# Merge gates of the LRU branch projected between its pairs of tiles, with a new scan cost and other engines for small copies, in a one-core trunk layer on Trainium2

## The chip, the cores and the metric

The kernel runs on one core of one Trainium2 chip. A core has five engines that run their own instruction queues in order: TensorE (PE in the profile; PEld is its weight load), VectorE (DVE), ScalarE (ACT), GpSimd (POOL) and SyncE (SP, which here only issues DMAs). The metric is the device time of one execution in microseconds (us), as the median of several runs. One execution is also recorded by the hardware profiler; its span goes from its first to its last instruction.

## The reference, cut to what matters

One layer of a streaming encoder works on 512 prompt rows and 128 sample rows (8 requests of 16), 640 in all, with 1024 channels, in float32:

```python
x = x + 0.5 * swiglu(rms_norm(x, norm_ffn1), w_ffn1_up, w_ffn1_down)      # d_ff 2816
h = rms_norm(x, norm_mix)
aq, ak, av, hq, hf, hi, hg, lx, lg, ga, gb, gc = split(h @ w_in)          # 10752 columns
A = sliding_window_attention(aq, ak, av)                # per head norms, sinks, caches
B = hgrn2(hq, hf, hi, hg)                               # gated linear recurrence
xc = causal_conv4(lx)                                   # depthwise, width 4
r, ig = sigmoid(xc @ w_a + b_a), sigmoid(xc @ w_x + b_x)     # 16 blocks of 64
a = exp(-8 * r * softplus(-lambda))
hs = scan(h[t] = a[t] * h[t-1] + sqrt(1 - a[t]**2) * (ig * xc)[t])
C = hs * gelu(lg)
merged = sigmoid(ga) * (A @ w_attn_o) + sigmoid(gb) * (B @ w_hgrn_o) + sigmoid(gc) * (C @ w_lru_o)
x = x + merged @ w_out
x = x + 0.5 * swiglu(rms_norm(x, norm_ffn2), w_ffn2_up, w_ffn2_down)
```

The outputs are the new rows, new keys and values, and the new states: of the convolution (its last three inputs), of the LRU (its last `hs`) and of B.

## The kernel before, in words

Activations lie transposed, 128 channels on the partitions and the 640 rows along the free dimension, two halves of 320. A float32 product is made of three matmuls of a rounded format: each operand is split into a high part and a low part (what is left), and high times high, high times low and low times high are summed. RA and RB (16 tiles of 128 x 640 each) hold the high parts (tiles 0 to 7) and the low parts (8 to 15) of whatever is multiplied next.

**A projection** (`proj`, L744 to L756) makes 128 output channels: a DMA on SP brings a weight tile `wr` (three slots); ACT or DVE casts it to `wh` (L750, two slots); DVE subtracts to `wl` (L751, two slots); then 48 matmuls of 320 columns (8 k-tiles, three parts, two halves; 24 where there are four k-tiles) go to two of four `pp` banks of PSUM, which DVE evacuates. Weight tiles get their slots strictly in the order in which the projections are issued in the program.

**The order of all work** is planned while the program is built. Every operation is entered in program order with its candidates of engines and a cost each, in us (`dve`, `act`, `pol`, L356 to L362). It gets a rank: the number of the current item (each `proj` raises it by 1, each `pair` by 2) plus `S.late`, ties by program order; `wr`, `wh` and `wl` rank at item minus 4, 2 and 1.5. `Sched.run` (L265) then repeatedly takes the engine whose next operation can start first by the estimated costs and gives it, among the operations that could start within 0.04 us of that, the one of lowest rank. The result is a fixed instruction order for each engine; on the chip each engine follows it and waits for its inputs.

**The stages**: first feed-forward (`ffn`, L891); attention with the gates `ga` (`attention`), and its merge, 8 projections with `w_attn_o`; the LRU branch (`lru`, L1169); the HGRN branch (`hgrn`, L1256, eight heads); `w_out`; second feed-forward.

**The feed-forward** works in chunks of the 22 tiles of d_ff: 4, 6, 6 and 6. The first chunk uses plain projections: four tiles of gate and value (8 projections), then 8 down projections of four k-tiles. The other chunks use `pair`, a form with 7 products instead of 8, which needs sums and differences of the normed input: `combos` (L777). A first part of these is entered after tile 0 with `S.late = 4` (L909 to L911). The second part, `rest()` (L812), writes over RA (or RB in the second feed-forward), so it must follow the last of the 8 up projections. It is entered at L912 to L913, right ahead of the 8 down projections, with no lateness: eight splits (a cast on ACT and a subtraction on DVE each, 128 x 640) and two subtractions.

**The LRU branch** treats eight tiles in four pairs. The four first tiles of `lx` are projected during attention. For each pair: projections of `lx` where missing; convolution on DVE (`xc`); the small copies to `CB`, which gathers the states to be output (L1192, L1193); splits, and 12 small matmuls a tile (`me`) against the block weights; sigmoids, exp and tanh on ACT; sqrt on ACT and products on DVE; the scan on DVE (L1227), entered in the plan at the cost of an elementwise operation over 640 elements; two more small copies to `CB` (L1229, L1230). Then, tile by tile, the `lg` projection, gelu on ACT, the product with `hs` and its split into RB (L1232 to L1237). After the last pair the states are transposed and put out, five merge gates are projected (`gate`, L947: a projection, a product with the norm's scale, a sigmoid, in one of six `mgC` slots), then the three projections of the first HGRN head (`heads(0)`), then the merge (L955): 8 projections with `w_lru_o`, the remaining three gates entered between them.

The small copies to `CB` may go to POOL or DVE (L1192, L1193, L1229, L1230). In an HGRN head, four copies of a 32 x 160 tile into the attention matrix may go to ACT or POOL (L1347).

Of the kernel before, what the change touches and what calls it, by code (L numbers as in the profile page):

```python
# [13 lines left out]
ALU = mybir.AluOpType  # L14
# [331 lines left out]
def trunk_kernel(ctx: ExitStack, tc: tile.TileContext, A: dict, O: list):  # L346
# [544 lines left out]
    def ffn(wu, wd, norm, R, H, sfx, done, aside=()):  # L891
        ops = None
        for f0, nf in CHUNKS:
            for f in range(nf):
                for at, job in aside:
                    if at == f0 + f:
                        job()
                if f0:
                    g, u = pair(wu, f0 + f, ops, sfx)
                else:  # L900
                    late = not sfx and f < 2
                    g = scaled("fA" + sfx, proj(wu, 0, KD, f * P, R), late)
                    fn(g.v, g.v, AF.Silu)
                    u = scaled("fB" + sfx, proj(wu, 0, KD, FF + f * P, R), late)
                tt(u.v, g.v, u.v, ALU.mult)
                parts(H, f, u.v)
                if f0 + f == ASIDE:
                    S.late = LATE
                    ops, rest = combos(norm, R, sfx)  # L909
                    S.late = 0.0  # L910
            if f0 == 0:  # L911
                rest()  # L912
            for m in range(KD):  # L913
                ps = proj(wd, f0 * P, nf, m * P, H)
                for o, p in halves(xk(m), ps):
                    stt(o, p, 0.5, o, ALU.mult, ALU.add)
                if f0 + nf == 22:
                    done(m)
# [247 lines left out]
    def smp(v):  # L1166
        return v[:, TP:T].r("p (b t) -> p b t", b=NB)

    def lru():  # L1169
        bds = [S.buf("bd") for _ in range(2)]  # L1170
        for b in bds:
            fill(b.v, 0.0)
        for j in range(4):
            xcs, rs, igs, las, lts = [], [], [], [], []
            for i in range(2):
                m = 2 * j + i
                y = early[m] if m < len(early) else branch(m)
                bd = bds[i]
                for w, nm_ in ((0, "lru_w_a"), (1, "lru_w_x")):
                    for h in range(2):  # L1180
                        a, b = h * 64, h * 64 + 64
                        dma(bd[a:b, w * P + a:w * P + b].at((w, h)), A[nm_][0, 2 * m + h])
                xc = S.buf("lc")
                fn(xc.v, y.v, AF.Identity, scale=prm(CVW + 24 + m), bias=prm(CVB + m))
                for t in range(3):
                    s = 3 - t
                    w = prm(CVW + t * 8 + m)
                    stt(xc[:, s:TP], y[:, 0:TP - s], w, xc[:, s:TP], ALU.mult, ALU.add)
                    stt(smp(xc.v)[:, :, s:], smp(y.v)[:, :, :SB - s], w, smp(xc.v)[:, :, s:], ALU.mult, ALU.add)
                    hist = HIST[:, m, 0:24].r("p (b j) -> p b j", b=NB)[:, :, t:]  # L1190
                    stt(smp(xc.v)[:, :, :s], hist, w, smp(xc.v)[:, :, :s], ALU.mult, ALU.add)
                cp(CB[:, m, 0:3].at(m), y[:, TP - 3:TP], only=("POOL", "DVE"))  # L1192
                cp(CB[:, m, 3:27].at(m).r("p (b j) -> p b j", b=NB), smp(y.v)[:, :, SB - 3:], only=("POOL", "DVE"))  # L1193
                r, ig = S.buf("lr"), S.buf("li")
                for h, l, x in ((BH.v, BL.v, bd.v), (NH.v, NL.v, xc.v)):
                    cp(h, x, only=("ACT",))
                    tt(l, x, h.cast(F32), ALU.subtract)
                for w, o, bias in ((0, r, BA), (1, ig, BX)):
                    for q in range(2):
                        ps = S.buf("me")  # L1200
                        mm([(ps[:, :HT], a[:, w * P:(w + 1) * P], hv(b.v)[:, q, :], a is BH and b is NH, a is BL)
                            for a, b in ((BH, NH), (BH, NL), (BL, NH))])
                        fn(hv(o.v)[:, q, :], ps[:, :HT], AF.Sigmoid, bias=prm(bias + m))
                tt(ig.v, ig.v, xc.v, ALU.mult)
                rs.append(r), igs.append(ig)
            hss = []
            for i in range(2):
                m = 2 * j + i
                a, t = S.buf("la"), S.buf("lt")
                fn(a.v, rs[i].v, AF.Exp, scale=der(N8SP, m))  # L1210
                fn(t.v, rs[i].v, AF.Tanh, scale=der(P8SP, m))
                q = rs[i]
                fn(q.v, a.v, AF.Square)
                stt(t.v, q.v, 1.0, t.v, ALU.add, ALU.mult)
                las.append(a), lts.append(t)
            for i in range(2):
                m = 2 * j + i
                a, t, ig = las[i], lts[i], igs[i]
                fn(t.v, t.v, AF.Sqrt)
                tt(t.v, t.v, ig.v, ALU.mult)  # L1220
                a0 = smp(a.v)[:, :, 0]
                sm = HIST[:, m, 24:32].at(m)
                tt(sm, a0, sm, ALU.mult, only=("DVE",))
                tt(smp(t.v)[:, :, 0], smp(t.v)[:, :, 0], sm, ALU.add, only=("DVE",))
                fill(a0, 0.0, only=("DVE",))
                hs = rs[i]
                S.op([dve(T, lambda o=hs.v, a=a.v, t=t.v: nc.vector.tensor_tensor_scan(o(), a(), t(), 0.0, op0=ALU.mult, op1=ALU.add))],  # L1227
                     [a.v, t.v], [hs.v])
                cp(CB[:, m, 27:28].at(m), hs[:, TP - 1:TP], only=("POOL", "DVE"))  # L1229
                cp(CB[:, m, 28:36].at(m), smp(hs.v)[:, :, SB - 1], only=("POOL", "DVE"))  # L1230
                hss.append(hs)
            for i in range(2):  # L1232
                m = 2 * j + i
                g = scaled("lg", proj(W, 0, KD, LG + m * P, RA))
                fn(g.v, g.v, AF.Gelu_apprx_tanh)
                tt(g.v, g.v, hss[i].v, ALU.mult)
                parts(RB, m, g.v)  # L1237
        co = S.buf("co")
        for h in range(2):
            ps = S.buf("ml")  # L1240
            tr([(ps[0:36, i * P:(i + 1) * P], CB[:, 4 * h + i, :], ident.v) for i in range(4)])
            cp(co[0:36, h * 512:(h + 1) * 512], ps[0:36, :], only=("ACT", "DVE"))
        dma(O[5], co[0:3, :])
        dma(O[10], co[3:27, :])
        dma(O[6], co[27:28, :])
        dma(O[11], co[28:36, :])
        more = lambda m: gate(GC, m, "mgC")
        gates = [more(m) for m in range(5)]
        pre.append(heads(0))
        merge(A["w_lru_o"][0], gates, more)  # L1250

# [4 lines left out]
    def hgrn():  # L1256
# [44 lines left out]
        def head(i):  # L1301
# [31 lines left out]
            for h in (2, 4, 8, 16, 32, 64):  # L1333
# [4 lines left out]
                if h < 32:  # L1338
                    mm([(ps[j * 32:j * 32 + 32, t * 16:t * 16 + 16], K[:, t * P + j * 32:t * P + j * 32 + 32],
                         blocks(Q[:, t * P + j * 32:t * P + j * 32 + 32], h)[:, :, 1, :], True, True) for t in range(n // P) for j in range(4)])  # L1340
                    dst = blocks(atc[:, :n // 4], h)[:, :, 1, :]
                    S.op([dve(n // 8, lambda d=dst, k=masks[h][:, :nb // 4, :], q=ps[:, :n // 8].r("p (n h) -> p n h", h=h):
                              nc.vector.copy_predicated(d(), k(), q()))], [ps.v, mk.v, atc.v], [dst])
                    if h == 16:
                        for j in range(4):
                            p = slice(j * 32, j * 32 + 32)
                            cp(a4[p, :, p].at(j), atc[p, :].r("p (t l) -> p t l", t=NT), only=("ACT", "POOL"))  # L1347
                elif h == 32:
                    mm([(ps[j * 32:j * 32 + 32, t * 32:t * 32 + 32], K[:, t * P + j * 32:t * P + j * 32 + 32],
                         Q[:, t * P + j * 32 + 32:t * P + j * 32 + 64], True, True) for t in range(4) for j in (0, 2)])  # L1350
                    for j in (0, 2):
                        p = slice(j * 32, j * 32 + 32)
                        cp(a4[p, 0:4, j * 32 + 32:j * 32 + 64].at((h, j)), ps[p, 0:P].r("p (t l) -> p t l", t=4), only=("ACT",))
                else:
                    mm([(ps[0:64, t * 64:t * 64 + 64], K[:, t * P:t * P + 64], Q[:, t * P + 64:t * P + P], True, True) for t in range(4)])
                    cp(a4[0:64, 0:4, 64:P].at(h), ps[0:64, 0:256].r("p (t l) -> p t l", t=4), only=("ACT",))
# [131 lines left out]
```

## Time and profile before

| what | before |
|---|---|
| median of 3 runs | 1921.0 us (1920.73 to 1923.34) |
| profiled execution, its time | 1923.28 us |
| its span | 1921.5 us |
| instructions | 35215 |
| PE busy | 1898.9 us (99%) |
| DVE busy | 1389.1 us (72%) |
| ACT busy | 735.8 us (38%) |
| POOL busy | 44.3 us (2%) |
| granted PE clock, mean | 0.996 |

In a row of the profile stand the line of the kernel, the engine, the operation, the tile written and the tiles read (`out<-in`), shapes and a count. AR is the arena in which most tiles of a stage lie, RW and RY are regions whose type changes with the stage, `me` and `ml` PSUM banks of small products, NL and NH the low and high part of the tile that is multiplied next, RS the norm's scale. Helpers record each operation under their own line: L369 is any product or sum of two tiles, L383 any fused multiply and add, L393 any activation or table load on ACT, L402 and L403 copies and casts on ACT and DVE, L405 copies on POOL, L438 any matmul. In brackets or after a bar stands idle time of the engine before the row, and what ended it. Matmuls overlap, so the time of one (0.31 us) is longer than the distance between two.

### The profile page before, as it was taken

To read this page: it belongs to the slowest core of one execution; us is meant where nothing else is said; L and a number is where in the kernel's file an instruction comes from. 1 tells how busy PE (TensorE), PEld (TensorE's weight loads), DVE (VectorE), ACT (ScalarE), POOL (GpSimd) and SP (SyncE) were. 2 spreads that over 40 slices of the span, in tenths; PEclk is the share of its full clock that TensorE was granted. 3 is DMA by queue.
4 is the path that set the end of the run, shared out by engine and by line. 5 is a ranking of instruction groups with operands and counts; after the bars stand their busy time and mean duration, and the time that the engine had idled before them with its cause. 6 is when DMAs were issued, how large, how long until landed. Compare 5 with 4: busy or idle time off the path is not lost.

```text
span 1921.5 us, 35215 instructions
## 1 busy us (share of the span) xinstructions
PE 1898.9 (99%) x14654; PEld 1853.0 (96%) x14654; DVE 1389.1 (72%) x2599; ACT 735.8 (38%) x1295; POOL 44.3 (2%) x86
## 2 busy tenths in 40 slices
PE   8999999999999999999999999999999999999999
PEld 8999999999999999999999999999999999999998
DVE  7897685877787773787547778877556978586784
ACT  6343251433478630876002344335112324142340
POOL 2000000000000000020000000000000000000000
PEclk9999999999999999999999999999999999999999
DMA  6232332224321212213222222222322133222322
GB/s 144 66 94 80 93 87 78 75 78 139 102 62 50 62 48 77 61 57 103 77 77 74 84 80 79 79 81 83 122 72 77 56 99 90 87 65 79 99 64 80
DMA packets 303488, 156.89 MB, mean 82 GB/s; under 512 B 21324, under 2 KB 300956, under 8 KB 303328
## 3 DMA queue, kind: packets, MB, share of 16 engines
q1 hardware_dynamic: 302576, 154.58, 27.7%
q8 instruction: 115, 1.88, 0.4%
q0 software_dynamic: 736, 0.06, 0.4%
q14 instruction: 45, 0.37, 0.1%
q10 hardware_dynamic: 16, 0.00, 0.0%
HBM read 143.32 MB, written 10.63 MB: 80 GB/s over the span
## 4 chain that ended last, share of the span: by engine, by line
PE 93%; DVE 4%; ACT 2%; issue 1%; DMA 1%; SPq 0%; ACTq 0%; DVEq 0%
PE pp L438 84%; PE me L438 4%; PE ml L438 3%; PE ml L447 1%; PE me L447 1%; DVE AR L383 1%; ACT AR L393 1%; DVE AR L369 1%; DVE RB L369 0%; DVE AR L1227 0%; ACT L393 0%; DMA RX<-in_x_prompt_dram 0%; DVE wl L751 0%; SPq L417 0%; DVE RA L369 0%
## 5 line engine op out<-in xcount | busy, mean ns | idle before, releaser
L438 PE MATMUL pp<-RA,wh 128*128 128x320 f32 x4192 | 815.0, 314 | 0.3 <-DVE AR L369 0.3
L438 PEld LDWEIGHTS pp<-RA,wh 128*128 128x128 f32 x4192 | 659.1, 189 | 13.1 <-issue 9.7
L438 PE MATMUL pp<-RA,wl 128*128 128x320 f32 x2096 | 490.7, 310 | 4.9 <-DVE wl L751 4.9
L438 PE MATMUL pp<-RB,wh 128*128 128x320 f32 x2016 | 389.0, 310 | 0.9 <-DVE AR L369 0.9
L438 PEld LDWEIGHTS pp<-RA,wl 128*128 128x128 f32 x2096 | 354.7, 188 | 5.9 <-DVE wl L751 5.9
L438 PEld LDWEIGHTS pp<-RB,wh 128*128 128x128 f32 x2016 | 320.4, 188 | 1.5 <-DVE AR L369 1.4
L750 DVE CAST wh<-wr 128x1024 fp32r<-128x1024 f32 (+2 forms) x142 | 89.4, 630 | 237.2 <-PE pp L438 236.5
L438 PE MATMUL pp<-RB,wl 128*128 128x320 f32 x1008 | 241.9, 310 | 1.6 <-DVE wl L751 1.6
L751 DVE TENSOR_TENSOR wl<-wr,wh 128x1024 fp32r<-128x1024 f32 (+2 forms) x196 | 216.7, 1106 | 1.6 <-ACT wh L750 1.0
L836 ACT CAST RW<-AR 128x512 fp32r<-128x512 f32 x180 | 110.4, 621 | 264.9 <-PE pp L438 135.0
L438 PEld LDWEIGHTS pp<-RB,wl 128*128 128x128 f32 x1008 | 172.1, 188 | 1.9 <-DVE wl L751 1.9
L369 DVE TENSOR_TENSOR AR<-AR 128x640 f32<-128x640 f32 (+12 forms) x272 | 140.0, 519 | 28.9 <-ACT AR L393 16.5
L369 DVE TENSOR_TENSOR AR<-pp,AR 128x320 f32<-128x320 f32 x268 | 127.6, 485 | 35.8 <-PE pp L438 32.7
L393 ACT ACTIVATE AR<-AR 128x640 f32<-128x640 f32 (+2 forms) x184 | 110.5, 604 | 96.9 <-DVE AR L369 89.6
L438 PE MATMUL pp<-RX,RW 128*128 128x320 f32 x864 | 138.6, 309 | 0.0
L438 PEld LDWEIGHTS pp<-RX,RW 128*128 128x128 f32 x864 | 129.6, 188 | 0.0
L833 DVE TENSOR_TENSOR RW<-AR,RW 128x512 fp32r<-128x512 f32 x180 | 122.3, 686 | 2.4 <-ACT RW L836 0.9
L393 ACT ACT_TABLE_LOAD x73 | 93.7, 1283 | 2.5 <-PEq L1476 1.4
L402 ACT COPY AR<-me 128x512 f32<-128x512 f32 (+3 forms) x72 | 25.8, 373 | 123.9 <-PE me L447 115.2
L383 DVE SCALAR_TENSOR_TENSOR AR<-pp,AR 128x320 f32<-128x320 f32 x128 | 61.3, 483 | 15.5 <-PE pp L438 15.4
L438 PE MATMUL pp<-RY,RW 128*128 128x320 f32 x432 | 69.2, 309 | 0.0
L750 ACT CAST wh<-wr 128x1024 fp32r<-128x1024 f32 (+1 forms) x54 | 53.7, 994 | 36.9 <-PE pp L438 36.5
(195 smaller groups left out, 1960.7 us busy)
## 6 DMA issues: line engine op xcount, KB each, us to landing
wr<-in_w_in_dram SPq DMA_DIRECT2D x84, 512.0 KB, 3.7
wr<-in_w_ffn_up_dram SPq DMA_DIRECT2D x52, 512.0 KB, 3.8
AR<-in_w_ffn_up_dram SPq DMA_DIRECT2D x36, 512.0 KB, 4.6
wr<-in_w_ffn_down_dram SPq DMA_DIRECT2D x48, 384.0 KB, 3.3
wr<-in_w_ffn_down_dram SPq DMA_DIRECT2D x16, 256.0 KB, 2.8
wr<-in_w_attn_o_dram SPq DMA_DIRECT2D x8, 512.0 KB, 3.7
AR<-in_state_hgrn_dram SPq DMA_DIRECT2D x8, 512.0 KB, 4.7
wr<-in_w_lru_o_dram SPq DMA_DIRECT2D x8, 512.0 KB, 3.8
```

What stands on the lines that cost most here:

```text
L369: alts = [dve(out.n, lambda: nc.vector.tensor_tensor(out(), a(), b(), op=op))]
L383: return S.op([dve(out.n, lambda: nc.vector.scalar_tensor_tensor(out(), a(), ap_of(s), b(), op0=op0, op1=op1), isinstance(s, View))], [a, ...
L393: nc.scalar.activation(out(), a(), func, bias=ap_of(bias), scale=ap_of(scale), **kw)
L402: alts = [act(out.n, lambda: nc.scalar.copy(out(), a()), 0, a), dve(out.n * (1.0 if a.in_psum else 0.5), lambda: nc.vector.tensor_copy(out ...
L438: nc.tensor.matmul(o(), l(), m(), start=s, stop=e)
L447: nc.tensor.transpose(o(), i(), d())
L750: S.op([act(nk * P, lambda: nc.scalar.copy(h(), r())), dve(nk * P * 0.5, lambda: nc.vector.tensor_copy(h(), r()))], [r], [h], lag=2)
L751: S.op([dve(nk * P, lambda: nc.vector.tensor_tensor(l(), r(), h().bitcast(F32), op=ALU.subtract))], [r, h], [l], lag=1.5)
L833: S.op([dve(out.n, lambda: nc.vector.tensor_tensor(out(), a(), b(), op=op))], [a, b], [out], lag=lag)
L836: S.op([act(out.n, lambda: nc.scalar.copy(out(), a()))], [a], [out], lag=lag)
```

## The change

1. Four of the five merge gates leave the place after the last pair: in each pair, after the `lg` tile 0 (`i == 0`) is entered, one gate is entered, ahead of the `lg` projection of tile 1. After the last pair the loop enters what is missing of five, which is one. `more` is defined ahead of the loop for this.
2. The scan's cost in the plan is that of 1280 elements instead of 640. The instruction is the same.
3. The four kinds of `CB` copies may go to ACT or DVE, and the copies of the attention tile in the HGRN heads to ACT or DVE; POOL gets none of these.
4. `rest()` is entered with `S.late = 4` in both feed-forward stages.

```diff
             if f0 == 0:
+                S.late = 4.0
                 rest()
+                S.late = 0.0
...
+        gates, more = [], lambda m: gate(GC, m, "mgC")
         for j in range(4):
...
-                cp(CB[:, m, 0:3].at(m), y[:, TP - 3:TP], only=("POOL", "DVE"))
-                cp(CB[:, m, 3:27].at(m).r("p (b j) -> p b j", b=NB), smp(y.v)[:, :, SB - 3:], only=("POOL", "DVE"))
+                cp(CB[:, m, 0:3].at(m), y[:, TP - 3:TP], only=("ACT", "DVE"))
+                cp(CB[:, m, 3:27].at(m).r("p (b j) -> p b j", b=NB), smp(y.v)[:, :, SB - 3:], only=("ACT", "DVE"))
...
-                S.op([dve(T, lambda o=hs.v, a=a.v, t=t.v: nc.vector.tensor_tensor_scan(o(), a(), t(), 0.0, op0=ALU.mult, op1=ALU.add))],
+                S.op([dve(2 * T, lambda o=hs.v, a=a.v, t=t.v: nc.vector.tensor_tensor_scan(o(), a(), t(), 0.0, op0=ALU.mult, op1=ALU.add))],
                      [a.v, t.v], [hs.v])
-                cp(CB[:, m, 27:28].at(m), hs[:, TP - 1:TP], only=("POOL", "DVE"))
-                cp(CB[:, m, 28:36].at(m), smp(hs.v)[:, :, SB - 1], only=("POOL", "DVE"))
+                cp(CB[:, m, 27:28].at(m), hs[:, TP - 1:TP], only=("ACT", "DVE"))
+                cp(CB[:, m, 28:36].at(m), smp(hs.v)[:, :, SB - 1], only=("ACT", "DVE"))
...
                 parts(RB, m, g.v)
+                if i == 0:
+                    gates.append(more(len(gates)))
...
-        more = lambda m: gate(GC, m, "mgC")
-        gates = [more(m) for m in range(5)]
+        while len(gates) < 5:
+            gates.append(more(len(gates)))
         pre.append(heads(0))
         merge(A["w_lru_o"][0], gates, more)
...
-                            cp(a4[p, :, p].at(j), atc[p, :].r("p (t l) -> p t l", t=NT), only=("ACT", "POOL"))
+                            cp(a4[p, :, p].at(j), atc[p, :].r("p (t l) -> p t l", t=NT), only=("ACT", "DVE"))
```

## The prediction, made before the changed kernel ran

> **What bounds the kernel now.** I read the page's busy line first, then the waits of the TensorE, then a table of stretches, and last the timeline where the waits lie.
>
> ```profile
> PE 1898.9 (99%) x14654; PEld 1853.0 (96%) x14654; DVE 1389.1 (72%) x2599; ACT 735.8 (38%) x1295; POOL 44.3 (2%) x86
> ```
> ```profile
> PE pp L438 <- DVE wl L751: 6.4, 5, 2.4
> PE me L447 <- DMA RX<-in_x_prompt_dram: 4.6, 2, 2.6
> PE me L438 <- DVE NL L369: 2.4, 1, 2.4
> ```
>
> TensorE (PE) is busy 99%, so only its gaps can be won. The largest sum is five waits for `wl`, the low part of a weight tile, which VectorE (DVE) writes; one wait for `NL` has the same length. The waits on DMA belong to the start, which the change leaves alone. What a gap costs is more than its idle time; the table of stretches shows it (columns: length, then busy us and count of PE, PEld, DVE, ACT, POOL; then the granted PE clock).
>
> ```profile
> 63.00:79.00 16.00, 14.41 (x100) 14.14 (x98) 13.38 (x22) 7.53 (x11) 0.00 (x0) 1.00 0.23 66
> 79.00:84.00 5.00, 5.00 (x23) 4.86 (x24) 4.60 (x12) 1.78 (x4) 0.00 (x0) 0.66 0.25 73
> 767.00:893.00 126.00, 120.34 (x792) 117.84 (x791) 100.20 (x188) 102.60 (x134) 18.45 (x26) 0.97 0.21 62
> 791.00:802.00 11.00, 8.22 (x35) 7.33 (x34) 10.76 (x18) 7.76 (x12) 3.72 (x4) 0.69 0.18 51
> 822.00:827.00 5.00, 2.62 (x18) 2.36 (x17) 5.00 (x10) 1.55 (x3) 0.53 (x2) 1.00 0.06 19
> 864.00:868.00 4.00, 3.55 (x21) 2.87 (x21) 4.00 (x9) 2.58 (x4) 2.63 (x3) 1.00 0.35 102
> 912.00:960.00 48.00, 48.00 (x329) 48.00 (x328) 26.32 (x39) 4.76 (x6) 0.00 (x0) 1.00 0.27 77
> 1522.00:1537.00 15.00, 13.28 (x91) 13.03 (x90) 12.34 (x21) 7.60 (x11) 0.00 (x0) 1.00 0.24 68
> 1537.00:1542.00 5.00, 5.00 (x24) 4.85 (x24) 3.48 (x7) 0.00 (x0) 0.00 (x0) 0.66 0.32 94
> ```
>
> 912 to 960 runs without a gap: 48 us for 329 matmuls, 0.1459 us each. At that pace the other stretches lost: 63 to 84, 21 less 123 x 0.1459 = 3.1 us; 1522 to 1542, 20 less 115 x 0.1459 = 3.2; 791 to 802, 11 less 35 x 0.1459 = 5.9; 822 to 827, 2.4; 864 to 868, 0.9. Together 15.5 us: 6.3 in the two feed-forward stages and 9.2 in the LRU stage (all of 767 to 893 lost 126 less 792 x 0.1459 = 10.4, so 1.2 lies in small pieces). The rows of 79 and 1537 are full of busy PE and still lost 1.6 and 1.5: the granted clock was 0.66 there, right after a gap. The Trainium skill's page "TensorE: Matmul & The Clock Gate" (section "What's actually happening") has the clock fall to half after an idle window of about 3.4 us; the gaps here are shorter (2.4 us at most, waits above), so its length does not fit, while its halving does, and by it no fall would be owed to these gaps.
>
> **The LRU stage, gate projections.** The timeline shows why PE starves (first three rows ACT, DVE and PE near the first pair, then the second pair):
>
> ```profile
> 784.39 1.05 ACT L750 CAST wh<-wr 128x1024 fp32r<-128x1024 f32 x1 [0.38 <-PE pp L438]
> 796.30 1.22 DVE L751 TENSOR_TENSOR wl<-wr,wh 128x1024 fp32r<-128x1024 f32 x1
> 794.72 0.64 PE L438 MATMUL me<-NL,BH 128*128 128x320 f32 x1 [2.41 <-DVE NL L369]
> ```
> ```profile
> 815.55 1.04 ACT L750 CAST wh<-wr 128x1024 fp32r<-128x1024 f32 x1
> 817.01 1.48 DVE L1227 TENSOR_TENSOR_SCAN AR<-AR 128x640 f32<-128x640 f32 x1
> 818.87 1.47 DVE L1227 TENSOR_TENSOR_SCAN AR<-AR 128x640 f32<-128x640 f32 x1
> 820.27 1.54 DVE L369 TENSOR_TENSOR AR<-AR 128x640 f32<-128x640 f32 x2
> 822.38 1.55 DVE L369 TENSOR_TENSOR RB<-AR,RB 128x640 fp32r<-128x640 f32 x2
> 824.09 1.22 DVE L751 TENSOR_TENSOR wl<-wr,wh 128x1024 fp32r<-128x1024 f32 x1
> 825.37 0.56 PE L438 MATMUL pp<-RA,wl 128*128 128x320 f32 x2 [2.38 <-DVE wl L751]
> ```
>
> The cast `wh` ends at 785.4, its `wl` starts at 796.3: it stood 11 us behind the first pair's scans, products and the next pair's convolution. At the second pair it waited from 816.6 to 824.1. A projection is 48 matmuls, 48 x 0.1459 = 7.0 us; its successor's weights may be converted only in that time, since there are two `wh` and two `wl`. Cast 1.04 and subtraction 1.22 leave 7.0 - 2.3 = 4.7 us of slack, less than either wait. So the order on DVE, not its amount, makes the gap.
>
> The plan gives a free engine the ready work of the lowest item number; `wl` ranks at its projection's item minus 1.5 (L751), the pair's work at the item reached when it was issued. Counted from the merge before, the fourth projection has `wl` at 2.5 both times. Before, it is LG3, and the second pair's convolution and the first pair's second product (item 2) come ahead; after, it is LG2, and both stand at item 3, behind. The seventh has 5.5: before it is LG4, behind the second pair's products (3 and 4); after, LX4, with one product (4) ahead and one (6) behind. And each pair hands PE 7.0 us more to run.
>
> What this adds is work for DVE and ACT in the stage (not in the kernel):
>
> ```profile
> L393 ACT ACT_TABLE_LOAD x24 | 30.8, 1283 | 0.4
> L751 DVE TENSOR_TENSOR wl<-wr,wh 128x1024 fp32r<-128x1024 f32 x15 | 18.2, 1215 | 0.0
> L369 DVE TENSOR_TENSOR RW<-pp,RS 128x320 f32<-128x320 f32 x3 | 1.4, 479 | 0.0
> L393 ACT ACTIVATE RW<-RW 128x640 f32<-128x640 f32 x1 | 0.7, 742 | 0.0
> L750 DVE CAST wh<-wr 128x1024 fp32r<-128x1024 f32 x6 | 4.2, 692 | 6.2 <-PE pp L438 6.1
> L403 DVE COPY CB<-AR 128x1 f32<-128x1 f32 x1 | 0.2, 153 | 0.0
> L403 DVE COPY CB<-AR 128x8 f32<-128x8 f32 x1 | 0.7, 715 | 0.0
> ```
> ```profile
> 878.68 0.88 PE me L438 x6
> 893.79 1.55 DVE L369 TENSOR_TENSOR RB<-AR,RB 128x640 fp32r<-128x640 f32 x2
> ```
>
> A gate costs DVE 1.215 + 2 x 0.479 + at most 0.692 = 2.9 us, four 11.5. The stage's PE time grows by 28 us and shrinks by the gaps: 126 + 28 - 9 = 145, DVE 100.2 + 11.5 + the copies (below, 4) = 116, 80% against 100.2/126 = 80% before; ACT 102.6 + 4 x 0.742 + up to 8 more table loads x 1.283 (a sigmoid between two gelus) + four casts of 1.04 + copies of 8 at most = 128, 88%. Neither becomes the bound by amount. Also moved: the four weight loads and their SP issues come earlier; the DMA share of 767 to 893 is 0.21, so they cost nothing. One gate (of the five) plus three head projections stay between LG7 and the merge, 4 x 7.0 = 28 us; the last pair's chain ran from its last small matmuls (`me`, to 879.6) to its products in RB (895.3), 16 us, so this cover holds; without it the merge would wait up to 16 us.
>
> **The scan's cost** in the plan (0.066 + 1.042 ns an element) goes from 0.73 to 1.40 us, against 1.48 measured. It adds no instruction; it makes the plan see the burst about as long as it is (two scans were 1.5 us short). I count it with the gates. Of the 9.2 us I take 8.3, leaving one stall of the smallest size (0.9); bounds: 3.3 (the first stays) and 10.4 (all).
>
> **Combinations later.** `rest()` overwrites RA (RB in the second layer half), so it starts when the last up projection has passed, exactly when the first down projections need weights:
>
> ```profile
> 1527.49 2.30 DVE L369 TENSOR_TENSOR RB<-RW,RB 128x640 fp32r<-128x640 f32 x3 [1.36 <-PE pp L438]
> 1531.91 0.42 DVE L750 CAST wh<-wr 128x512 fp32r<-128x512 f32 x1
> 1534.51 0.82 DVE L369 TENSOR_TENSOR AR<-AR 128x640 f32<-128x640 f32 x1
> 1535.98 0.68 DVE L751 TENSOR_TENSOR wl<-wr,wh 128x512 fp32r<-128x512 f32 x1
> 1536.72 0.56 PE L438 MATMUL pp<-RA,wl 128*128 128x320 f32 x2 [1.72 <-DVE wl L751]
> ```
>
> The second `wl` was possible at 1532.3 and came at 1536.0, behind four combination steps and others. With rank item + 4 the combinations stand behind the next weights. `wl` at 1532.3 to 1533.1 ends before PE needs it (1536.72 - 1.72 = 1535.0). Late next is the last product: 1534.5, or 1534.2 now, plus its own 0.8, a cast of 0.7 on ACT and a subtraction of 0.8 gives 1536.6; PE has 18 matmuls of the second projection, until 1535.0 + 2.6 = 1537.6. The displaced steps, about five of 0.8 us, fit between the down projections before the first pair needs them some 25 us later (8 projections of 24 matmuls, 28 us). If that cover were gone, PE would wait those 4 us. I take 5.6 of the 6.3 (0.35 each for a step of 0.8 that is already running); bounds 0 and 6.3.
>
> **Copies off POOL.** 26 `CB` copies and 16 of the attention tile go to ACT or DVE:
>
> ```profile
> L405 POOL COPY AR<-AR x16: 318/402/714, 1021.7 to 1317.1; 32x160 f32<-32x160 f32 x16
> L402 ACT COPY AR<-AR 32x160 f32<-32x160 f32 x16 | 5.2, 324 | 33.7 <-DVE AR L1343 33.6
> 1008.00:1340.00 332.00, 332.00 (x3799) 307.13 (x3798) 255.46 (x504) 130.05 (x218) 6.52 (x16) 1.00 0.28 80
> ```
>
> A `CB` copy on DVE is 0.15 us (0.715 once, beside other work), on ACT nearest 0.324: 4 to 8 us, counted above. The sixteen, 16 x 0.324 = 5.2 us, lie in a stage where PE has no idle time in 332 us and DVE is 77% busy. Value 0 for the time; without the cover 5.2, and a gain is bounded by 16 x (0.402 - 0.324) = 1.2. A changed order elsewhere: between -1.5 and +1.5, taken as 0.
>
> **Sum.** The profiled execution took 1923.3, of which 1921.5 is the span and 1.8 lies around it. 1921.5 - 8.3 - 5.6 = 1907.6, or 1909.4 around; that execution lies 2.3 over the median 1921.0 of three, so the median should be 1907.1.
>
> **Rivals.** (A) The feed-forward stall only moves: DVE was busy 13.38 of 16 us and 12.34 of 15 before the gap, and non-preemptive steps of 0.8 still collide. Against: it has slack behind (3.48 of 5). Then 1907.1 + 5.6 = 1912.7. (B) The LRU burst stays: the scans and products still outrank `wl`, and the first gap of 5.9 comes in another place, 1913. For: DVE 10.76 of 11 busy there. Against: the ranks above, and PE's extra 7.0 us per pair. (C) Nothing happens: the plan finds the same waits in both, 1920 to 1921. (D) Slower: each gate's sigmoid brings two table loads and holds ACT's queue 2 x 1.283 + 0.742 = 3.3 us, and the casts `wh` queue behind. It decides once a hold with the work before it exceeds the slack of 4.7; four such stalls at the price of the first gap, 4 x 5.9, give 1907.1 + 23.6 = 1930.7. Against: 0.4 us of idle before 24 loads, so a load costs its 1.283 only. The skill's page "ScalarE: Activation LUTs" ("What ACT_TABLE_LOAD costs") adds a drain of 1.38 to each; by it the hold would be 6.1, past the slack, and (D) would be likely; the row above contradicts it. (E) The clock falls come from elsewhere and stay: then only idle time is won. The clock losses are 1.6 + 1.5 in the two rows at 0.66, and 5.9 less 2.78 idle = 3.1 at 791; 1907.1 + 6.2 = 1913.3. Against: the three rows under 1.00 each touch a gap.
>
> **How the numbers follow.** Forecast 0.63 (its own range 1903.5 to 1911), A 0.12, B 0.13, C 0.05, D 0.04, E 0.03. The range 1903.5 to 1914 starts at 1921.0 - 10.4 - 6.3 - about 1 of order, and takes in A, B and E; C and D are out. 0.2% is 3.8 us, what this kernel's measurement can tell (its three runs spread 2.6). Faster is all but C and D, 0.90 with a little left for both going half wrong; same 0.06, slower 0.04.
>
> **What would show it.** Right: no wait of PE for `wl` or `NL` above 1 us between 767 and the merge, the clock 1.00 there and after the last up projection of both feed-forward stages, the stage from 767 to the last LRU scan longer by about 20 us with the merge after it earlier by 8. Wrong: an idle PE behind ACT loads (D), behind the last product in the feed-forward (A), or a scan burst with a waiting `wl` (B); or the HGRN stage (332 us) longer by over 1 us.

## The result, and the profile after

| what | before | after |
|---|---|---|
| median | 1921.43 us (4 runs, 1920.73 to 1923.34) | 1910.36 us (4 runs, 1909.01 to 1910.46) |
| profiled execution | 1923.28 us, span 1921.5 | 1910.45 us, span 1908.2 |
| TensorE (PE) busy | 1898.9 us | 1892.1 us |
| POOL instructions | 86 | 44 |
| granted PE clock, mean | 0.996 | 0.999 |

The ratio is 0.9939, with a 95% interval of 0.9922 to 0.9956: 11.1 us faster in the medians, 13.3 us in the spans of the two profiles. The forecast was 1907.1 us, in a range of 1903.5 to 1914.

PE's busy time fell by 6.8 us though its 14654 matmuls are the same: matmuls at half clock count as busy, and in the profile of before the clock was at half for 13.7 us in all, which is a loss of 6.8. The page after, and PE's waits after (us in total, times, longest):

```profile
PE 1892.1 (99%) x14654; PEld 1847.3 (97%) x14654; DVE 1388.2 (73%) x2613; ACT 746.0 (39%) x1325; POOL 20.5 (1%) x44
```
```profile
PE me L447 <- DMA RX<-in_x_prompt_dram: 4.4, 2, 2.9
PE ml L447 <- DMA AR<-in_norm_ffn_dram: 2.8, 1, 2.8
PE pp L438 <- DVE AR L383: 2.0, 4, 0.6
PE pp L438 <- DVE AR L369: 1.2, 2, 0.9
...
PE pp L438 <- DVE wl L751: 0.3, 1, 0.3
```

The waits for `wl` went from 6.4 us to 0.3 and that for `NL` is gone. New are four waits, 2.0 us together, for L383: there DVE adds a down projection to the residual and so frees its PSUM banks. Where the time went is read from small matmuls that mark the stages; the first and the last start of each stand after the durations, of before and then of after:

```profile
L438 PE MATMUL me<-NL,BH x32: 302/309/635, 767.1 to 879.1; 128*128 128x320 f32 x32
L438 PE MATMUL me<-NL,ones x20: 303/309/309, 463.1 to 1481.7; 128*128 128x320 f32 x20
L438 PE MATMUL me<-NL,bd x20: 304/310/318, 474.8 to 653.2; 128*128 128x320 f32 x20
```
```profile
L438 PE MATMUL me<-NL,BH x32: 302/309/318, 765.5 to 891.4; 128*128 128x320 f32 x32
L438 PE MATMUL me<-NL,ones x20: 302/309/309, 461.3 to 1470.2; 128*128 128x320 f32 x20
L438 PE MATMUL me<-NL,bd x20: 304/312/318, 473.0 to 651.5; 128*128 128x320 f32 x20
```

With two more marks (the first wait for `wl`, which ends the start, and the first masked copy of an HGRN head) this gives stretches, which I use for every run below:

| kernel | start | first feed-forward (to first `bd`) | attention (to first `BH`) | LRU (to first masked copy) | HGRN, `w_out` (to last `ones`) | second feed-forward | span |
|---|---|---|---|---|---|---|---|
| before | 22.0 | 452.8 | 292.3 | 246.8 | 467.8 | 439.8 | 1921.5 |
| after | 22.0 | 451.0 | 292.5 | 237.0 | 467.7 | 438.0 | 1908.2 |

The LRU stretch gained 9.8 us, each feed-forward 1.8, and nothing else moved by more than 0.2. The stretches with the stalls of before run without a gap in the LRU stage (length, busy us and count of PE, PEld, DVE, ACT, POOL, then the clock; the last row is where the first feed-forward stalled before):

```profile
765.00:902.00 137.00, 137.00 (x933) 136.47 (x932) 105.65 (x198) 106.64 (x153) 0.90 (x3) 1.00 0.24 69
790.00:803.00 13.00, 13.00 (x91) 13.00 (x90) 12.19 (x23) 7.95 (x14) 0.00 (x0) 1.00 0.14 40
820.00:832.00 12.00, 12.00 (x84) 12.00 (x83) 11.69 (x20) 6.90 (x13) 0.00 (x0) 1.00 0.25 71
77.00:86.00 9.00, 7.91 (x51) 7.16 (x50) 8.72 (x23) 3.68 (x6) 0.00 (x0) 1.00 0.27 80
```

What DVE does around the first pair's scans, from the timeline after:

```profile
784.53 1.22 DVE L751 TENSOR_TENSOR wl<-wr,wh 128x1024 fp32r<-128x1024 f32 x1
...
788.68 1.48 DVE L1230 TENSOR_TENSOR_SCAN AR<-AR 128x640 f32<-128x640 f32 x1
...
790.74 1.48 DVE L1230 TENSOR_TENSOR_SCAN AR<-AR 128x640 f32<-128x640 f32 x1
...
795.03 1.22 DVE L751 TENSOR_TENSOR wl<-wr,wh 128x1024 fp32r<-128x1024 f32 x1
796.17 0.82 DVE L369 TENSOR_TENSOR NL<-AR,NH 128x640 fp32r<-128x640 f32 x1
```

`wl` passes before the scans and again among the products; before, one `wl` stood behind the whole burst until 796.3. `NL` comes later than before (793.85 then), and PE does not wait for it: it has a projection to run until 797.8.

### The profile page after: what moved, and what is told of

Same layout as the page of the kernel before. It is cut to its first block, busy times and chain, and to the rows that moved or that the text cites. A ratio compares the mean times of both kernels' runs of the same rounds, so it can differ in the third digit from the quotient of the medians.

```text
span 1908.2 us, 35178 instructions
## 1 busy us (share of the span) xinstructions
PE 1892.1 (99%) x14654; PEld 1847.3 (97%) x14654; DVE 1388.2 (73%) x2613; ACT 746.0 (39%) x1325; POOL 20.5 (1%) x44
## 4 chain that ended last, share of the span: by engine, by line
PE 95%; DVE 2%; ACT 1%; DMA 1%; issue 0%; SPq 0%; DVEq 0%; ACTq 0%
PE pp L438 86%; PE me L438 4%; PE ml L438 3%; PE ml L447 1%; PE me L447 1%; DVE RB L369 0%; DMA RX<-in_x_prompt_dram 0%; DVE RA L369 0%; DVE AR L369 0%; DVE AR L383 0%; ACT AR L393 0%; DVE wl L751 0%; SPq L417 0%; ACT AR L402 0%; DVE RW L383 0%
## 5 line engine op out<-in xcount | busy, mean ns | idle before, releaser
L369 DVE TENSOR_TENSOR AR<-AR 128x640 f32<-128x640 f32 (+12 forms) x272 | 140.1, 519 | 34.8 <-ACT AR L393 22.4
L750 ACT CAST wh<-wr 128x1024 fp32r<-128x1024 f32 (+2 forms) x59 | 58.1, 985 | 63.1 <-PE pp L438 59.1
L383 DVE SCALAR_TENSOR_TENSOR AR<-pp,AR 128x320 f32<-128x320 f32 x128 | 61.2, 484 | 15.5 <-PE pp L438 15.5
L438 PE MATMUL pp<-RA,RW 128*128 128x320 f32 x432 | 66.3, 309 | 0.0
```

The costliest lines, as they stand in the source:

```text
L369: alts = [dve(out.n, lambda: nc.vector.tensor_tensor(out(), a(), b(), op=op))]
L383: return S.op([dve(out.n, lambda: nc.vector.scalar_tensor_tensor(out(), a(), ap_of(s), b(), op0=op0, op1=op1), isinstance(s, View))], [a, ...
L438: nc.tensor.matmul(o(), l(), m(), start=s, stop=e)
L750: S.op([act(nk * P, lambda: nc.scalar.copy(h(), r())), dve(nk * P * 0.5, lambda: nc.vector.tensor_copy(h(), r()))], [r], [h], lag=2)
```

## The experiments

Twelve more kernels were profiled, one of them the kernel before again. Where no number of runs is given, there is one execution. The stretches of all of them:

| kernel | start | first ff | attention | LRU | HGRN, out | second ff | span |
|---|---|---|---|---|---|---|---|
| e1_gates | 21.3 | 451.2 | 292.0 | 238.9 | 467.6 | 438.9 | 1909.9 |
| e2_scan | 21.1 | 451.2 | 291.9 | 247.0 | 467.7 | 438.3 | 1917.2 |
| e3_late | 21.2 | 451.1 | 292.4 | 246.6 | 467.7 | 438.0 | 1917.0 |
| e4_copies | 20.6 | 451.2 | 292.0 | 244.6 | 467.6 | 438.3 | 1914.3 |
| e5_rank | 20.4 | 451.2 | 292.2 | 244.1 | 467.7 | 438.3 | 1913.9 |
| e6_lowrank | 22.0 | 451.1 | 292.4 | 242.8 | 467.6 | 438.0 | 1913.9 |
| e7_twoscans | 21.9 | 451.1 | 292.1 | 244.0 | 467.6 | 438.0 | 1914.7 |
| e8_rest_after | 21.3 | 450.3 | 291.9 | 237.0 | 467.5 | 437.7 | 1905.7 |
| e9_noscan | 22.3 | 451.0 | 292.0 | 238.3 | 467.7 | 438.5 | 1909.8 |
| e10_nocopies | 20.7 | 451.1 | 292.3 | 237.8 | 467.6 | 438.0 | 1907.5 |
| e11_before_again | 22.4 | 452.7 | 292.3 | 246.9 | 467.6 | 439.8 | 1921.7 |
| e12_best | 21.5 | 450.4 | 292.7 | 236.9 | 467.7 | 436.2 | 1905.4 |

**The gates alone** (before, with this):

```diff
+        gates, more = [], lambda m: gate(GC, m, "mgC")
...
+                if i == 0:
+                    gates.append(more(len(gates)))
...
-        more = lambda m: gate(GC, m, "mgC")
-        gates = [more(m) for m in range(5)]
+        while len(gates) < 5:
+            gates.append(more(len(gates)))
```

> Only the four gates between the pairs are moved; scan cost, copies and the combinations stay as before. If the place of the gates is what removed the LRU stalls (the theory: the weights that PE needs next rank ahead of the pair's own work, and PE has 7.0 us more to run per pair), the stage from the first small LRU matmuls to the first HGRN mask copy gains at least 8 of the 9.9 us that the whole change gained there: span 1911 to 1913. If the true scan cost in the plan is needed as well, one or two stalls of 2 us with a clock fall remain: span 1915 to 1919.

Measured: 1911.83 us (4 runs), ratio 0.995 (0.9935 to 0.9964), span 1909.9, LRU 238.9. The place of the gates alone makes 7.9 of the LRU stretch's 9.8 us, just under the 8 expected; one wait of 0.41 us for `NL` and two of 0.2 to 0.3 us for ACT remain. The span lies below the forecast because the feed-forwards were shorter too, though their code is that of before; e2 and e11 show why.

**The scan's cost alone.**

```diff
-                S.op([dve(T, lambda o=hs.v, a=a.v, t=t.v: ...
+                S.op([dve(2 * T, lambda o=hs.v, a=a.v, t=t.v: ...
```

> Only the scan's cost in the plan is changed. Theory: ranks are unchanged and the plan is greedy, so the scans and products still run ahead of the waiting weights; the three stalls stay within 1 us each, span 1920 to 1922. Rival (the plan misjudged the burst only because two scans were 1.5 us short): the stalls shrink by 1.5 us each and at least one clock fall goes, span 1914 to 1917.

Measured: span 1917.2, LRU 247.0 against 246.8: nothing, as the theory said, and the waits stay:

```profile
PE pp L438 <- DVE wl L751: 6.6, 5, 2.6
...
PE me L438 <- DVE NL L369: 2.4, 1, 2.4
```

The span is 4.3 us shorter all the same. The order up to the end of the first feed-forward is that of before, the gap there is as long (1.60 us against 1.59), but the clock did not fall. The table of stretches, of before and of this run:

```profile
77.00:86.00 9.00, 7.41 (x39) 7.00 (x38) 8.11 (x19) 3.15 (x5) 0.00 (x0) 0.81 0.21 60
1531.00:1544.00 13.00, 11.28 (x66) 10.88 (x65) 11.24 (x21) 2.18 (x3) 0.00 (x0) 0.87 0.14 42
```
```profile
77.00:86.00 9.00, 7.93 (x53) 7.79 (x54) 8.59 (x26) 2.86 (x5) 0.00 (x0) 1.00 0.26 78
1531.00:1544.00 13.00, 11.29 (x76) 10.88 (x75) 10.40 (x20) 1.45 (x2) 0.00 (x0) 1.00 0.21 61
```

The clock stood at 1.00, and more matmuls fit in the same time (53 against 39, 76 against 66; the gaps lie some tenths apart, so the stretches of the table, 1.6 and 1.5 us shorter, are the better measure). A clock fall costs about 1.6 us and does not come with every gap.

**The later combinations alone.**

```diff
+                S.late = 4.0
                 rest()
+                S.late = 0.0
```

> Only the combinations are later, in both feed-forward stages. Theory: it gains what the whole change gained outside the LRU stage, 1.7 us in the first and 1.8 us in the second, span 1918.0; what is left of the stall is PE waiting for the evacuation of the first two down projections. Rival (the feed-forward gain came from other edits or from the order they cause): span 1920 to 1922.

Measured: 1920.16 us (10 runs), ratio 0.9992 (0.9982 to 1.0001), span 1917.0. The span agrees with the first theory by coincidence: against e1, e2, e4 and e5, which lack this edit and had no clock fall there (451.2; 438.3 or 438.9), the first feed-forward (451.1) gained 0.1 us and the second (438.0) 0.3 to 0.9. The other 1.6 and 1.5 us by which it is shorter than in the profile of before are that profile's clock falls. The idle time moved more than it went; PE's rows in this run:

```profile
81.15 0.42 PE L438 MATMUL pp<-RB,wh 128*128 128x320 f32 x1 [0.49 <-DVE AR L383]
82.15 0.71 PE L438 MATMUL pp<-RB,wh 128*128 128x320 f32 x3 [0.58 <-DVE AR L383]
```

**The copies alone**: `only=("ACT", "DVE")` at the four `CB` copies and at the attention tile.

> Only the small copies are taken off GpSimd. Theory: nothing waits for them, PE hides them, span 1921.5 within 1 us, the HGRN stage the same within 0.5 us. Rival (GpSimd's copies block VectorE's two-input operations, or the copies' ends hold up a tile): span 1916 to 1920, with VectorE's rows of 128x640 products shorter in the LRU stage.

Measured: span 1914.3, LRU 244.6. The theory missed: 2.2 us went from the LRU stretch (3.1 more went with the clock falls of the feed-forwards and 1.4 with a shorter start). The rival's mechanism does not show either: the scan took 1474 to 1502 ns before and 1473 to 1487 here, the products of 128x640 took 817 ns on average in both, and in the kernel before nothing waited for a copy on GpSimd. What went is the second stall; the plan came out in another order:

```profile
820.00:832.00 12.00, 11.81 (x81) 11.55 (x80) 12.00 (x25) 7.88 (x11) 0.00 (x0) 1.00 0.30 86
```

81 matmuls where before had 66. The first stall stayed (2.54 us for `NL`, with the clock at half for 6.8 us around it, as before). That the order and not GpSimd is the cause was not shown by a run of its own; e10 bounds what the copies are worth in the changed kernel.

**The rank of the weights alone**: the kernel before, with earlier ranks inside `lru`.

```diff
+        S.lags = (6, 5.5, 5)            # in lru(); elsewhere (4, 2, 1.5)
-        dma(r, w[...], lag=4)   ...  [h], lag=2)   ...  [l], lag=1.5)
+        dma(r, w[...], lag=lr)  ...  [h], lag=lh)  ...  [l], lag=ll)
```

> The kernel before, with the gates after the pairs as before, but inside the LRU branch the weight parts rank earlier: DMA, cast and subtraction at item minus 6, 5.5 and 5 instead of 4, 2 and 1.5. If the rank of the weights alone makes the gaps, PE's idle time between the first small LRU matmul and the HGRN branch falls from 5.6 us to under 1.5 us, and the stretch from that matmul to the first mask copy of HGRN is 237 to 239 us, as with the gates moved. Rival (without the gates' 28 us PE has too little to run while VectorE works through a pair): the waits for wl go, but PE waits instead for NL or the sigmoids, idle time 3 us or more, stretch 243 to 247 us.

Measured: LRU 244.1, the rival's case. In the LRU stage no wait for `wl` is left, and PE waits for the other side of the burst instead:

```profile
796.02 0.42 PE L439 MATMUL me<-NL,BH 128*128 128x320 f32 x1 [0.38 <-DVE NL L370]
...
830.75 0.41 PE L439 MATMUL me<-NH,BH 128*128 128x320 f32 x1 [2.72 <-ACT NH L403]
831.92 0.64 PE L439 MATMUL me<-NL,BH 128*128 128x320 f32 x1 [0.75 <-DVE NL L370]
```

Giving the weights the way lets PE finish its projections sooner and stand before `me` with nothing else to run. PE is idle for 4.7 us in this stretch, against 5.6 before. The stretch is 2.7 us shorter, but order alone removed only 0.9 us of idle time: the rest is mostly that the clock was at half for 3.4 us here and for 6.8 us in the profile of before.

**The gates with the weights one item later**: the changed kernel, `S.lags = (4, 2, 0.5)` in `lru`.

> The changed kernel, gates between the pairs, but inside the LRU branch the subtraction of the weights ranks one item later (item minus 0.5). If the rank is what counts, waits for wl come back: 2 us or more of idle PE in the LRU branch, stretch to the first mask copy 240 to 246 us instead of 237.0. Rival (the extra PE work per pair covers the burst whatever the order): under 0.5 us idle, stretch 237 to 238 us.

Measured: LRU 242.8, as expected; 5.8 us of the 9.8 are lost again. Of these 2.8 are idle time, and most of the rest is a clock at half from 793.1 to 799.9. The wait is named `NL`, not `wl` as I had written, but `wl` is what was missing: without it PE had no projection to run until `NL` came. DVE's row, then PE's:

```profile
794.10 1.22 DVE L753 TENSOR_TENSOR wl<-wr,wh 128x1024 fp32r<-128x1024 f32 x1
```
```profile
792.85 0.45 PE L439 MATMUL me<-NL,BH 128*128 128x320 f32 x1 [2.07 <-DVE NL L370]
```

In the changed kernel a `wl` passed at 784.5, ahead of both scans. So neither part does it alone: e5 has the rank without the work and keeps 4.7 us of idle time, e6 the work without the rank and keeps 2.8; with both there is none.

**Each scan twice**, in the changed kernel:

```diff
                 S.op([dve(2 * T, ... tensor_tensor_scan ...)], [a.v, t.v], [hs.v])
+                S.op([dve(2 * T, ... tensor_tensor_scan ...)], [a.v, t.v], [hs.v])
```

> The changed kernel with each of the eight scans done twice (same inputs, same output), in the plan at the same cost again: 8 x 1.48 = 11.9 us more of VectorE in the LRU branch, 80% to 88% busy by the prediction's count. If VectorE's amount is no bound there, the stretch grows by under 1.5 us (237.0 to 238.5) though the burst is 3 us longer. Rival (VectorE is close to the bound, or the longer burst alone brings the stalls back): 240 us or more, with waits of PE for wl or NL of 2 us.

Measured: LRU 244.0, 7.0 us more for 11.9 us more of DVE. The rival's stretch came, its waits of 2 us did not: the clock stayed at 1.00 and no wait in the stage is above 0.81 us; they are many small ones, 4.4 us in all (the first row holds 0.3 us of the start):

```profile
PE pp L438 <- DVE wl L751: 2.0, 4, 0.8
...
PE pp L438 <- DVE RY L369: 1.3, 2, 0.8
PE pp L438 <- DVE RW L369: 0.7, 1, 0.7
```

DVE was busy 110.13 us of the 140 from 765 to 905, 79%, so it was not full. That points to the longer burst, which PE must outlast, and not to the amount; the run changes both and does not separate them.

**The late combinations behind the last product**, in the changed kernel:

```diff
-                S.late = 4.0
-                rest()
+                S.late = 6.0
+                rest((H[:, 8 + nf - 1, :].at(8 + nf - 1),))
...
-                    put(ops[name], q, x(h, n, q))
+                    put(ops[name], q, x(h, n, q), after if name == "x22" else ())
-                put(ops["t1"], q, x(0, 1, q))
+                put(ops["t1"], q, x(0, 1, q), after)
```

`after` is only one more read in the plan.

> The changed kernel; in the plan the second half of the late combinations (the splits of x22 and t1) may not start before the first chunk's last product is split, and the lateness is 6 instead of 4. Theory (the late combinations still fill VectorE just ahead of that product, so its split and the first evacuations come 1 us late): PE's waits for the evacuation after the first two down projections, 0.50 + 0.59 and 0.34 + 0.59 us in the changed kernel, fall to under 0.4 us in each half, span 1906.0 to 1907.5. Rival (the wait is the latency of the last product itself): the waits stay within 0.2 us, span 1907.8 to 1908.6. Third: the displaced splits come too late for the first pair and PE waits there, 1909 or more.

Measured: 1908.26 us (4 runs), ratio to before 0.993 (0.9914 to 0.9947), span 1905.7, feed-forwards 450.3 and 437.7. The span lies just below the theory's 1906.0; of the 2.5 us by which it is shorter than in the changed kernel, 1.0 lies in the feed-forwards and 1.3 in start and attention. In each the first wait for the evacuation is gone, the second stays at 0.59 us, above the 0.4 I had set:

```profile
81.48 0.70 PE L438 MATMUL pp<-RB,wh 128*128 128x320 f32 x3 [0.59 <-DVE AR L383]
```

So about half of that wait came from combinations ahead of the last product, and half stays.

**The changed kernel without the scan's cost** (`dve(T, ...)` again).

> The changed kernel with the scan's old cost in the plan (half of what it takes). The gates alone gave an LRU stretch (first small matmul to first mask copy of HGRN) of 238.9 us, the whole change 237.0. If the scan's cost makes that 1.9 us, the stretch is 238 to 239.5 with 0.5 to 1 us of idle PE; if the copies make it, 237.0 to 237.5.

Measured: LRU 238.3. The cost that did nothing in the old order is worth 1.3 us in the new one; the idle time that comes back is 0.41 us for `NL` and 0.32 us behind ACT.

**The changed kernel without the copies' new engines.**

> The changed kernel with the small copies on GpSimd or VectorE as before. Alone the copies gave 2.2 us in the LRU stretch, by one stall less. If that came from another order and the gates remove the same stall anyway, the stretch is 237.0 to 237.6. If the copies make the last 1.9 us (of the gates' 238.9), it is 238 to 239.5.

Measured: LRU 237.8, between the two cases: 0.8 us. Single parts make 7.9 (gates), 0 (scan) and 2.2 (copies), taken out of the whole 1.3 (scan) and 0.8 (copies): the gates' place does most, and what the others add depends on it.

**The kernel before, once more.**

> The kernel before, profiled a second time. If the halved clock after a gap depends on where the gap falls in a window that runs by itself, the same gaps (1.6 us in each feed-forward, 2.4 us twice in the LRU stage) show another number of halved windows of 3.4 us than the four of the first profile, each worth 1.7 us: one to three, span 1915 to 1920 with the same idle times. Rival (the clock fall belongs to the gap): four windows again, span 1920.5 to 1922.

Measured: span 1921.7, all stretches after the start within 0.2 us of the first profile (the start is 0.4 us longer), with the same clock falls; the expectation missed, and the rival's number held. But the run could not tell the two apart, as the clock in slices of 0.1 us shows, first of before, then of e2 (the clock is the third number from the end):

```profile
80.30:80.40 0.10, 0.10 (x2) 0.10 (x2) 0.10 (x2) 0.00 (x0) 0.00 (x0) 0.83 1.13 241
83.70:83.80 0.10, 0.10 (x2) 0.10 (x1) 0.06 (x1) 0.00 (x0) 0.00 (x0) 0.60 0.57 174
793.70:793.80 0.10, 0.00 (x0) 0.00 (x0) 0.10 (x1) 0.10 (x1) 0.10 (x1) 0.76 0.00 0
1537.80:1537.90 0.10, 0.10 (x3) 0.10 (x2) 0.10 (x1) 0.00 (x0) 0.00 (x0) 0.79 0.56 164
```
```profile
792.10:792.20 0.10, 0.10 (x2) 0.10 (x2) 0.10 (x1) 0.10 (x1) 0.00 (x0) 0.57 0.00 0
822.80:822.90 0.10, 0.10 (x3) 0.10 (x2) 0.10 (x2) 0.00 (x0) 0.00 (x0) 0.68 0.23 72
```

The clock steps from 1.00 to 0.50 or back within each slice, so the slice's mean gives the moment. In the profile of before the falls begin at 80.37, 793.75 and 1537.86, and the first ends at 83.78, after 3.41 us. The beginnings lie 713.39 and 1457.49 us apart, which is 209 and 427 times 3.413; the two falls of e2 lie 30.72 us apart, 9 times 3.413. In e11 the falls are again 209 and 427 such steps apart. So the falls of one execution lie on a grid of 3.41 us, and not at a fixed distance from their gaps: they come 2.99, 1.44 and 2.86 us after the gap begins. In e11 the first gap began 2.90 us before its fall, against 2.99 in the first profile. The grid lay nearly the same way against the kernel both times, by luck, so both cases would have given the same falls.

That the fall does not belong to the gap is shown by e1, e2, e4 and e5: they have the same first feed-forward with the same gap and no fall. Of the gaps of 1.6 to 1.7 us in the two feed-forwards, four of four were followed by a fall in the profiles of before and none of eight in those four kernels, while the second LRU gap of before, 2.4 us long, had no fall in either profile. Where a gap lies in time thus seems to decide, and not its length alone. Which place on the grid brings a fall stays open: carried back, the grid of e2 has points at 75.31 and 78.73, and its gap from 76.47 to 78.07 lay wholly between two points, as did that of before (77.38 to 78.97, between 76.95 and 80.37).

**A better version**: e8, with the second feed-forward's first tile evacuated without the norm's scale.

```diff
-                    late = not sfx and f < 2
+                    late = f < (1 if sfx else 2)
```

> The changed kernel with the splits of x22 and t1 after the last product (as in the run before, span 1905.7), and in the second feed-forward the first tile's two projections are evacuated without the norm's scale, which is multiplied in afterwards, as the first feed-forward does it for two tiles. Theory: PE's wait of 0.89 us for the norm's scale at the start of the second feed-forward goes, span 1904.5 to 1905.3, time 1906.5 to 1908. Rival: the added product on VectorE (0.8 us each) delays weights there, 1905.7 or more.

Measured: 1907.7 us (5 runs), ratio to before 0.9921 (0.9908 to 0.9935), span 1905.4. The wait of 0.89 us is gone and the second feed-forward takes 436.2 us, 1.5 less than in e8 (what made the other 0.6 stays open). The span fell by 0.3 only and lies 0.1 above the range, since start and attention were 1.0 us longer in that execution. Its interval overlaps that of e8 and that of the changed kernel; by the stretches it is the fastest of all.

## Why the prediction was right, and where not

**The place and the cause of the gaps: right.** The prediction had 9.2 us in three LRU stalls, put down to the order on DVE, and took 8.3 for the edit; it brought 9.8, inside the bounds of 3.3 and 10.4 (gates, scan cost and combinations without the copies, e10: 9.0). Both halves of its reason were needed: the rank (e6 without it: 242.8) and PE's extra 7.0 us per pair (e5 without it: 244.1, against 237.0). Rival B did not come. In one point the size was luck: 3.1 of the 5.9 us of the first stall were a clock at half, counted as sure. In both profiles of before and in e4 it lasted two steps of 3.41 us, in e2 and e3 one.

**"Neither becomes the bound by amount": right, with less room than it sounded.** DVE is busy 105.65 of 137 us, 77%, and ACT 106.64, 78%; e7 shows that 11.9 us more in DVE's bursts would have cost 7.0.

**ACT's table loads: right by more than counted.** Up to 8 more loads were allowed for; the group of loads in the LRU stage has one more, again with 0.4 us of idle time before all of them (24 loads before):

```profile
L393 ACT ACT_TABLE_LOAD x25 | 32.1, 1283 | 0.4
```

The instruction behind a load starts as soon as it ends: a load at 783.87 ends at 785.15, and the next instruction starts at 785.16. So rival D had no ground: the loads cost their 1.283 us and no drain on top. The Trainium skill's page "ScalarE: Activation LUTs" (section "What ACT_TABLE_LOAD costs") adds 1.38 us of drain to each; this trace has no room for it.

**The feed-forward: the step that failed.** 5.6 us were forecast. The profiles differ by 3.6, and e3 alone is 1.4 us faster in the medians, with an interval that reaches no change. Two errors lie in the step. First, of the 6.3 us to be won 3.1 were losses by the clock, counted as sure with the gap. They are not: eight such gaps had none. Second, "late next" was named as the last product alone. It came in time within some tenths, and then the third down projection was late: the first two end together, both waiting for the last product's part, and hold all four PSUM banks until DVE has evacuated one. The timeline after, second feed-forward, DVE and then PE:

```profile
1525.10 0.82 DVE L369 TENSOR_TENSOR RA<-AR,RA 128x640 fp32r<-128x640 f32 x1
...
1527.51 0.48 DVE L383 SCALAR_TENSOR_TENSOR AR<-pp,AR 128x320 f32<-128x320 f32 x1
...
1528.51 0.88 DVE L383 SCALAR_TENSOR_TENSOR AR<-pp,AR 128x320 f32<-128x320 f32 x2
```
```profile
1528.05 0.41 PE L438 MATMUL pp<-RA,wh 128*128 128x320 f32 x1 [0.34 <-DVE AR L383]
1529.05 0.71 PE L438 MATMUL pp<-RA,wh 128*128 128x320 f32 x3 [0.59 <-DVE AR L383]
```

That is rival A for the idle part. Its reason against, slack behind the stall, did not count, since the next to be late was a bank and not a weight.

**The scan and the copies at nothing of their own: right within the bounds for the whole, wrong for the copies alone.** Taken out of the whole, the copies are worth 0.8 us (e10), inside the 1.5 allowed for a changed order; the scan's cost, counted with the gates, 1.3 (e9). Alone the copies gave 2.2 (e4), by a stall that the new order removed.

**Rival E: half true.** Every clock fall touches a gap, so removing the gaps removed the falls; but a gap has one only at times.

**From the span to the median: the largest error.** The span was forecast at 1907.6 and came at 1908.2, with 1.5 us too little from the LRU and 2.0 too much from the feed-forward; that these two nearly cancel is luck. The median was forecast 2.3 us lower than the profiled execution, as before; the profile after lies at its own median (1910.45 against 1910.36). The surplus of the first profile was probably in part its clock falls, which the change removes: I took them off once as a gain and once more as the distance to the median. The first profile's mean clock was 0.996; in the seven executions of the kernel before that were timed beside e5 to e8, the span goes from 1917.7 us at a clock of 0.999 to 1922.0 at 0.996.

**What would show it**: the waits in the LRU stage, the clock of 1.00 and the unchanged HGRN stretch came as written. The stage from the first small matmul to the last scan grew by 13 us (889.3 less 767.1, then 900.9 less 765.5), not by about 20 (why stays open), and the stretch up to HGRN shrank by 9.8, not 8.

## What to carry to other kernels

Where an in-order engine feeds the engine that is the bound, a gap needs two remedies at once: independent work for the bound engine beside the burst, and an order that lets the next operand pass before the burst. After removing one wait, list every resource that the same instant holds (here the PSUM banks), not only the data. Where the clock falls after gaps, a single profile has them by luck: price idle time as sure, the fall as a chance, and compare stage by stage over several profiles before carrying a number to the median.

## What was not expected of the hardware

A gap of PE of 1.6 us was followed by a stretch at half clock in two profiles (0.81 granted over 77 to 86 us) and by none in four others with the same order and the same gap (1.00). The halved stretch lasted 3.41 us and cost 1.5 to 1.6 us each time. The halved stretches of one execution begin on a grid of 3.41 us (209, 427 and 9 steps apart, above). The Trainium skill's page "TensorE: Matmul & The Clock Gate" (section "What's actually happening") says that the clock is set by a window of 3.4 us that runs by itself and does not start with the kernel. That fits this grid, and falls that depend on where the gap lies; that only an idle window as long as that brings a fall does not fit gaps of 1.6 us. The start of the kernel, up to PE's first wait for `wl`, varied from 20.4 to 22.4 us between executions; PE's longest waits in it are for the DMAs of the first inputs.
